# A fourth group of seven products in each feed-forward block, and weights split by whole tiles into buffers of their own

## The chip, the core and the metric

The kernel runs on one NeuronCore of a Trainium2 chip. The metric is the device time of one execution in microseconds (us). The engines work side by side, each through its own queue in program order: TensorE (PE) multiplies matrices into the PSUM banks, VectorE (DVE) and ScalarE (ACT) work on tiles element by element, GpSimd (POOL) and SyncE (SP) mostly issue DMAs here.

## The reference

Two layers, 256 tokens, width 1024, all in float32. Each layer is a feed-forward block, an attention block and a second feed-forward block:

```python
def swiglu(h, w_gate, w_up, w_down):
    return (jax.nn.silu(h @ w_gate) * (h @ w_up)) @ w_down
...
for l in range(DEPTH):
    x = x + 0.5 * swiglu(rms_norm(x, ffn1_norm[l]), ffn1_w_gate[l], ffn1_w_up[l], ffn1_w_down[l])
    h = rms_norm(x, mix_norm[l])
    proj = h @ w_in[l]                      # 2304 columns: windowed and differential attention
    ...
    x = x + jnp.concatenate([out_a, out_b], axis=-1) @ w_out[l]
    x = x + 0.5 * swiglu(rms_norm(x, ffn2_norm[l]), ffn2_w_gate[l], ffn2_w_up[l], ffn2_w_down[l])
return rms_norm(x, final_norm)
```

The feed-forward width is 2816: five groups of 512 columns (groups 0 to 4) and a rest of 256. There are four such blocks in the kernel, numbered 1 to 4 here in order of time.

## The kernel before

**Exact products from rounded parts.** Each float32 operand is split in two: a high part, cast to the matmul type (by ScalarE, `act.copy`), and a low part, the operand less the high part (by VectorE, `tensor_tensor` with subtract). A product is the sum of three matmuls: high by high, low by high, high by low. So each weight that is loaded costs ScalarE a cast and VectorE a subtract before TensorE can use it. `emit_split` does that.

**Steps of weights.** The list `specs` holds the weights in order of use, one `Step` for 1 MB (a raw tile of 128 x 2048 float32, 8 KB in each partition, `N_RAW` = 6 of them). A step is split in two halves of 128 x 1024. Each half takes two tiles of 4 KB (high, low) out of one pool, `s4`, of `N_S4` = 28, which holds the activations too (`blk`). `weights()` takes the next step, and calls `ahead`, which issues loads, splits and preparations of later steps, up to `look[0]` half steps further on: 8 in the feed-forward blocks, 6 in attention (`IN_FFN`, `IN_MIX`).

**A plain group** of 512 columns: 24 matmuls for each of four weight steps (gate and up, 512 rows each), 96 in all; Silu of gate on ScalarE, times up on VectorE (`hidden`). The group before is turned by TensorE (`turn`: eight transposes, then a split) and goes through two down steps (`down`, 24 matmuls each).

**A group of seven** (`by_seven`; groups 2, 3 and 4, `SEVEN`) computes gate and up as one 2 by 2 product of blocks (two blocks of tokens, two halves of the rows) with seven block products in place of eight, 12 matmuls each. Their weights are: a (gate, upper rows), b (up, upper rows), d, c (gate and up, lower rows), and the sums b + c, a + b, a + b + c, a + b + c + d, built in order in the tiles of b and a. The two additions of `gather` are DMAs that POOL issues and that add into the raw tile. The two of `plus` are VectorE additions of two raw tiles, in halves. So each group has nine steps, in the order of TensorE's work: p1 (a), p7 (b + c), p2 (d), p3 (c), the first down step, p5 (a + b), p6, p4, the second down step. VectorE then combines the products (`put`), and ScalarE applies Silu to g0 and g1. The activations need four sums too (`make_sums`), made once a block.

**The order in a block**: group 0 plain, group 1 plain, groups 2 to 4 by seven, the rest of 256 columns, the last down steps (`ffn_end`, `ffn_close`).

Outside attention all engines keep the program's order (`kept`), so what `ahead` emits is the order of VectorE and ScalarE.

Of the kernel before, what the change touches and what calls it, by code (L numbers as in the profile page):

```python
# [14 lines left out]
P = 128  # L15
# [13 lines left out]
N_RAW, N_S4 = 6, 28  # L29
IN_FFN, IN_MIX = 8, 6  # L30
SEVEN = (2, 3, 4)
# [3 lines left out]
def trunk(ctx: ExitStack, tc: tile.TileContext, x, n1, g1, u1, d1, nm, w_in, sink,  # L35
# [56 lines left out]
    class Step:  # L92
        def __init__(self, kn, n, moves, key=None, prep=None, src=None, free=None, behind=None):
# [21 lines left out]
    def seven(wg, wu, c0, downs):  # L115
# [21 lines left out]
        return [Step(4, 512, load(a), key=a, free=[]),  # L137
                Step(4, 512, load(b), key=b, behind=gather(c, b), prep=gather(b, a)),
                Step(4, 512, load(d), key=d, free=[]),
                Step(4, 512, load(c), key=c, free=[]),  # L140
                downs[0],
                Step(4, 512, None, src=a, free=[]),
                Step(4, 512, None, prep=plus(c, a), src=a, free=[c]),
                Step(4, 512, None, prep=plus(d, a), src=a, free=[a, d]),
                downs[1]]

    def emit_dma(i):
# [9 lines left out]
        if s.behind is not None:  # L157
            s.behind()
# [52 lines left out]

    def ahead(n):

        n = min(n, 2 * len(specs) - 1)
        while True:
            if at["split"] <= n and at["prep"] > at["split"] // 2:
                for _ in emit_split(*divmod(at["split"], 2)):
                    pass
                at["split"] += 1
            elif at["prep"] <= min(n // 2 + 1, len(specs) - 1) and at["dma"] > at["prep"] and \  # L220
                    (specs[at["prep"]].prep is None or at["split"] >= 2 * at["prep"]):
                if specs[at["prep"]].prep is not None:
                    specs[at["prep"]].prep()
                at["prep"] += 1
            elif at["dma"] < min(at["use"] + AHEAD, len(specs)) and (specs[at["dma"]].moves is None or len(raws) < N_RAW):
                if specs[at["dma"]].moves is not None:
                    for _ in emit_dma(at["dma"]):
                        pass
                at["dma"] += 1
            else:  # L230
                break
# [11 lines left out]
    for l in range(DEPTH):  # L243
        def ffn_specs(wg, wu, wd):
            down = lambda g, h: plain(wd[l], h * 512, 512, 4 * g, 4)
            for k0 in (0, 4):
                specs.extend(plain(w[l], 0, 512, k0, 4) for w in (wg, wu))
            for g in range(1, NGRP):
                downs = [down(g - 1, h) for h in range(2)]
                if g in SEVEN:  # L250
                    specs.extend(seven(wg[l], wu[l], g * 512, downs))
                else:
                    specs.extend(plain(w[l], g * 512, 512, k0, 4) for w in (wg, wu) for k0 in (0, 4))
                    specs.extend(downs)
# [24 lines left out]
        for k0 in (0, 2):  # L279
            def o_moves(t, k0=k0, wo=wo):  # L280
                return [(t[g * 64:g * 64 + 64], wo[g * 256 + k0 * 64:g * 256 + (k0 + 2) * 64].rearrange("(k p) n -> p k n", p=64))
                        for g in range(2)]
            specs.append(Step(2, D, o_moves))
        fine.update(range(mixed + 2, len(specs)))
# [5 lines left out]
    class Norm:  # L290


        def __init__(self, g0, sums=len(SEVEN) > 0):
# [39 lines left out]
        def make_sums(self):  # L333
# [5 lines left out]
            def make(x, y, op):  # L339
# [4 lines left out]
                act.copy(sm[:, :, 0:P], v)  # L344
                dve.tensor_tensor(sm[:, :, P:S], v, f(sm[:, :, 0:P]), op=ALU.subtract)
# [3 lines left out]
            s1 = make(b1, t1, ALU.subtract)  # L349
            yield  # L350
            s2 = make(s1, t0, ALU.add)
            yield
            make(t1, t0, ALU.subtract)
            yield
            make(b0, s2, ALU.subtract)
# [12 lines left out]
        def stats(self, n=512):  # L368
# [7 lines left out]
            dve.tensor_scalar_mul(self.hr, self.r, 0.5)  # L376

# [189 lines left out]
    def ffn(norm, aside=None, before=None, final=False):  # L567
# [31 lines left out]
        def by_seven(h, g):  # L599

# [6 lines left out]

            m1, m7 = flat(), flat()
            act.copy(m1, prod(norm.quarter(0, 0), weights()))
            act.copy(m7, prod(norm.summed(2), weights(held=True)))  # L610
            hT = turn(h, 2)
# [6 lines left out]
            p5 = prod(norm.summed(0), weights())  # L618
            late = g == max(SEVEN)
            p6 = prod(norm.summed(1), weights(look[0] - 5 if late else 0, late))  # L620
            u2 = put(flat(), p6, m1, ALU.subtract)
            u3 = put(m7, m7, u2, ALU.add)
            p4 = prod(norm.quarter(1, 1), weights(look[0] - 4 if late else 0, late))
            g1 = put(m1, p4, u3, ALU.subtract)
            w = weights(look[0] - 3 if late else 0)
            silu(g1, g1, 1)
            put(u3, u3, p5, ALU.subtract)
            put(u2, u2, p5, ALU.subtract)
            put(u2, u2, p3, ALU.add)
            up(h, u2, g0, 0)  # L630
            up(h, u3, g1, 1)
            down(hT, g - 1, 1, w)
            return h

        def turn(hs, n):
            out_ = []
            for i in range(n):
# [11 lines left out]
        def down(hT, g, h, w):  # L649
            tokens(accs[h], [None] * (2 * g) + hT, w, 4 * g, last=(FC - 1, G4 - 1) if final and h else FC - 1)  # L650

# [13 lines left out]
        tokens(gs, norm.xs, weights(), 4)  # L665
        g = gate(gs)
        tokens(us, norm.xs, weights(), 4)
        h = hidden(g, us)
        for n in range(1, NGRP):
            sums = norm.make_sums() if n + 1 == min(SEVEN, default=0) else iter(())  # L670
            if n in SEVEN:
                look[0] = IN_FFN - max(0, n - 2) if before is not take_x else IN_MIX
                h = by_seven(h, n)
                continue
            gs = [bank(), bank()]
            tokens(gs, norm.xs, weights(), 0)
            hT = turn(h, 2)
            norm.copies()
            tokens(gs, norm.xs, weights(), 4)
            g = gate(gs)  # L680
            next(sums, None)
            us = [bank(), bank()]
            for k0 in (0, 4):
                tokens(us, norm.xs, weights(), k0)
                next(sums, None)
            h = hidden(g, us)
            for hh in range(2):
                down(hT, n - 1, hh, weights())
                if hh == 0:
                    next(sums, None)  # L690

        gu = [bank(), bank()]
        tokens(gu, norm.xs, weights(), 0)
        hT = turn(h, 2)
        tokens(gu, norm.xs, weights(), 4)
        h = hidden(gate([b[:, 0:256] for b in gu]), [b[:, 256:512] for b in gu])
        if aside is not None:
            aside()
        return accs, hT, lambda: turn(h, 1)

    BY_TOKENS = [(k, t) for t in range(2) for k in range(2)]
    G4 = 4 * (NGRP - 1)

    def ffn_end(parts, last):

        accs, hT, rest = parts
        hT = [None] * (2 * (NGRP - 1)) + hT
        hE = []
        look[0] = IN_MIX
        w = {0: weights()}  # L710

        def group(h, order, a=None, c=slice(None), first=0):
            tokens(a or accs[h], hT, w[h], G4, first=first, last=last[h], order=order, cols=c)

        def tail(h, order=BY_TOKENS, a=None, c=slice(None)):
            tokens(a or accs[h], [None] * (2 * NGRP) + hE, w["rest"], 4 * NGRP, last=last[h], order=order, cols=c, h=h)

        group(0, [(k, t) for k in range(3) for t in range(2)])
        hE.extend(rest())
        group(0, [(3, t) for t in range(2)])  # L720
        w["rest"] = weights()
        w[1] = weights(2)
        return group, tail

    def ffn_close(parts, nxt):
        group, tail = ffn_end(parts, (FC - 1, G4 + 3))
        res = Residual(nxt, parts[0])
        group(1, [(0, t) for t in range(2)])
        tail(0)
        for t in range(2):  # L730
            res.add(0, t)
        tail(1)
        ahead(2 * at["use"] - 2 + look[0])
        group(1, [(1, t) for t in range(2)])
# [330 lines left out]
```

## Time and profile before

| | |
|---|---|
| median of 3 runs | 935.24 us (934.86 to 935.65) |
| profiled execution | 935.0 us, span 933.2 us |
| TensorE busy | 921.1 us, 4796 matmuls and transposes |
| VectorE busy | 759.9 us, 1074 instructions |
| ScalarE busy | 566.8 us, 889 instructions |
| DMA packets | 194.58 MB, mean 208 GB/s |
| 12 groups of seven | POOL issues 24 adding DMAs, median 10.5 us to landing |

The span is the profiled stretch from the first to the last instruction; the execution's time has 1.8 us more around it. All instructions carry line 50 (a helper issues them), so they are told apart by their tiles: `raw` is a loaded weight, `w` a part of a split one, `s` an `s4` tile, `ps` a PSUM bank. In a timeline a row has the start, the time and, in brackets, how long the engine stood before it and what ended that.

### The profile page before, as it was taken

How to read it: one execution, taken by the hardware profiler on the slowest of the kernel's cores; microseconds unless marked ns; L12 is line 12 of the kernel's file. 1: busy time of each engine (PE TensorE's matmuls, PEld its weight loads, DVE VectorE, ACT ScalarE, POOL GpSimd, SP SyncE). 2: the span in 40 equal slices, each digit the busy share in tenths (PEclk: the TensorE clock that was granted, in tenths of full speed). 3: DMA queues.
4: the chain of work that ended last, by engine and by line, in shares of the span. 5: the costliest groups of instructions: out<-in, count | busy, mean ns of one | idle time of the engine just before them, and what ended most of it. 6: DMA issues, size and time to landing. Idle time of an engine off the chain costs nothing.

```text
span 933.2 us, 12665 instructions
## 1 busy us (share of the span) xinstructions
PE 921.1 (99%) x4796; PEld 780.7 (84%) x4796; DVE 759.9 (81%) x1074; ACT 566.8 (61%) x889; POOL 55.0 (6%) x73
## 2 busy tenths in 40 slices
PE   8999999999999999999999999999999999999997
PEld 6888878799898888888888888888999888888886
DVE  6759999869866588999776799996697566799994
ACT  7837576457745657576475466565577476466561
POOL 0400000000000001000000000000000000001011
PEclk9999999999999999999999999999999999999999
DMA  9996898827335858797767597887462367597831
GB/s 334 347 233 200 251 271 270 235 97 217 131 93 178 271 135 261 191 269 271 240 236 204 140 299 203 238 283 218 144 187 91 136 213 198 145 299 203 248 113 46
DMA packets 110893, 194.58 MB, mean 208 GB/s; under 512 B 3566, under 2 KB 31280, under 8 KB 110832
## 3 DMA queue, kind: packets, MB, share of 16 engines
q1 hardware_dynamic: 96528, 166.74, 52.8%
q0 software_dynamic: 12928, 25.46, 15.4%
q10 hardware_dynamic: 1376, 1.57, 0.5%
q8 instruction: 37, 0.61, 0.3%
q14 instruction: 24, 0.20, 0.1%
HBM read 192.71 MB, written 1.05 MB: 208 GB/s over the span
## 4 chain that ended last, share of the span: by engine, by line
PE 93%; DVE 4%; issue 1%; DMA 0%; ACT 0%; POOLq 0%; POOL 0%; ACTq 0%; DVEq 0%
PE ps L50 93%; DVE w L50 3%; DVE s L50 1%; DMA xk<-in_x_dram 0%; DVE tmp L50 0%; DVE raw L50 0%; ACT w L50 0%; DVE distA L50 0%; DVE xk L50 0%; DVE distB L50 0%; POOLq L1060 0%; POOL rf L50 0%; ACTq L50 0%; DVE lsum L50 0%; DVEq L50 0%
## 5 line engine op out<-in xcount | busy, mean ns | idle before, releaser
L50 PE MATMUL ps<-w,s 128*128 128x512 f32 (+1 forms) x2754 | 641.3, 391 | 1.2 <-DVE s L50 1.1
L50 PEld LDWEIGHTS ps<-w,s 128*128 128x128 f32 x2754 | 511.3, 188 | 107.5 <-DVE s L50 1.6
L50 DVE TENSOR_TENSOR w<-raw,w 128x1024 fp32r<-128x1024 f32 (+1 forms) x440 | 460.4, 1093 | 59.3 <-ACT w L50 58.1
L50 ACT CAST w<-raw 128x1024 fp32r<-128x1024 f32 (+1 forms) x440 | 391.1, 948 | 91.9 <-DVE raw L50 69.6
L50 PE MATMUL ps<-w,q 128*128 128x512 f32 x432 | 101.9, 389 | 0.0
L50 PEld LDWEIGHTS ps<-w,q 128*128 128x128 f32 x432 | 81.1, 188 | 16.8
L50 PE MATMUL ps<-s,w 128*128 128x256 f32 x672 | 84.0, 285 | 0.0
L50 PEld LDWEIGHTS ps<-s,w 128*128 128x128 f32 x672 | 81.7, 191 | 1.1
L50 ACT ACTIVATE s<-ps,gcol 128x256 fp32r<-128x256 f32 (+1 forms) x80 | 31.5, 488 | 47.0 <-PE ps L50 47.0
L50 DVE TENSOR_TENSOR raw<-raw,raw 128x1024 f32<-128x1024 f32 x48 | 56.5, 1219 | 0.0
L50 ACT CAST s<-ps 128x512 fp32r<-128x512 f32 x48 | 26.1, 593 | 46.5 <-PE ps L50 46.5
L50 POOL DMA_DIRECT2D raw<-in_ffn_w_up_dram x24 | 31.1, 1296 | 352.9 <-DVE w L50 166.5
L50 DVE TENSOR_TENSOR s<-ps,s 128x512 fp32r<-128x512 f32 x48 | 31.0, 684 | 25.1 <-ACT s L50 25.1
L50 PE MATMUL ps<-ident,s 128*128 128x128 f32 x304 | 39.9, 274 | 0.6 <-DVE s L50 0.6
L50 PEld LDWEIGHTS ps<-ident,s 128*128 128x128 f32 x304 | 35.0, 141 | 5.9 <-DVE s L50 1.4
L50 ACT ACTIVATE tmp<-tmp,r 128x512 f32<-128x512 f32 x24 | 17.3, 722 | 34.0 <-DVE tmp L50 34.0
L50 ACT ACTIVATE s<-s,negm 128x256 f32<-128x256 f32 x64 | 31.9, 500 | 6.3 <-DVE negm L50 6.1
L50 PE MATMUL ps<-w,v 128*128 128x512 f32 x144 | 34.6, 389 | 0.0
L50 ACT CAST q<-tmp 128x512 fp32r<-128x512 f32 x20 | 12.4, 621 | 35.3 <-DVE tmp L50 35.2
L50 PEld LDWEIGHTS ps<-w,v 128*128 128x128 f32 x144 | 27.0, 188 | 5.6
L50 DVE SCALAR_TENSOR_TENSOR s<-ps,gcol,s 128x256 fp32r<-128x256 f32 x48 | 20.3, 478 | 12.5 <-ACT s L50 12.4
L50 ACT COPY tmp<-ps 128x512 f32<-128x512 f32 x24 | 14.0, 584 | 22.6 <-PE ps L50 22.5
(106 smaller groups left out, 427.0 us busy)
## 6 DMA issues: line engine op xcount, KB each, us to landing
raw<-in_ffn_w_down_dram SPq DMA_DIRECT2D x44, 1024.0 KB, 5.4
raw<-in_ffn_w_gate_dram SPq DMA_DIRECT2D x39, 1024.0 KB, 6.0
raw<-in_ffn_w_up_dram SPq DMA_DIRECT2D x39, 1024.0 KB, 5.4
raw<-in_ffn_w_up_dram POOLq DMA_DIRECT2D x24, 1024.0 KB, 10.5
raw<-in_w_in_dram SPq DMA_DIRECT2D x14, 1024.0 KB, 5.1
raw<-in_ffn_w_gate_dram SPq DMA_DIRECT2D x8, 512.0 KB, 6.4
raw<-in_ffn_w_up_dram SPq DMA_DIRECT2D x8, 512.0 KB, 7.3
raw<-in_w_in_dram SPq DMA_DIRECT2D x8, 512.0 KB, 6.3
```

The source lines that it names most:

```text
L50: ins = issue(*a, **k)
```

## The change

- Group 1 goes by seven as well. The rest of 256 columns moves to the place between group 0 and group 1, and `make_sums` stands around it. The order of the block is: group 0, the rest, groups 1 to 4 by seven, then the rest's down step (`tail`) and the last two.
- The 28 shared tiles become 8 tiles of 8 KB for weights (tag `w`, `N_W`), and 12 of 4 KB for activations. A step takes two of the 8 KB tiles, one high and one low, and so four steps fit. The steps of the groups of seven and the down steps but the last two are `whole`: one cast and one subtract of 128 x 2048.
- `plus` adds a whole raw tile in one instruction.
- The order in which steps are split is decided by a model of the times (`clk`, `chain`, `fill`, `passed`), and `take` looks no further than the step itself. The loads have an order of their own (`order`).
- The adding DMA into b is held until the statistics of the norm are there (`held`, `flush`).

```diff
-N_RAW, N_S4 = 6, 28
-IN_FFN, IN_MIX = 8, 6
-SEVEN = (2, 3, 4)
+N_RAW, N_W, N_S4 = 6, 8, 12
+IN_FFN, IN_MIX = N_W - 1, N_W - 1
...
         def plus(x, to):
             def prep():
-                for h in (0, 2):
-                    x_, t_ = [raws[i][:, h:h + 2] for i in (x, to)]
-                    dve.tensor_tensor(t_, t_, x_, op=ALU.add)
+                dve.tensor_tensor(raws[to], raws[to], raws[x], op=ALU.add)
             return prep
...
         if s.behind is not None:
-            s.behind()
+            behind.append(s.behind)
+            if not held[0]:
+                flush()
...
-            loaded[i] = Split(i)
-        shape = (P, 8, P) if s.n == 256 else (P, 2, 512)
-        hi, lo = [s4.tile(list(shape), F32R, tag="s4", name=nm_("w")) for _ in range(2)]
-        loaded[i].parts.append((hi, lo))
+            loaded[i] = w = Split(i)
+            shape = {256: (P, 2, 8, P), 512: (P, 2, 2, 512), D: (P, 2, 2, 512)}[s.n]
+            w.both = [wp.tile(list(shape), F32R, tag="w", bufs=N_W, name=nm_("w")) for _ in range(2)]
+            if s.whole:
+                hi, lo = [t.rearrange("p a k n -> p (a k) n") for t in w.both]
+                act.copy(hi, raw)
+                dve.tensor_tensor(lo, raw, f(hi), op=ALU.subtract)
+        loaded[i].parts.append([t[:, j] for t in loaded[i].both])
+        if s.whole:
...
+    def fill(until):
+
+        while clk["dve"] < until and at["split"] < min(2 * at["use"] + LIVE, 2 * len(specs)) and act_once(at["split"]):
+            pass
+        while load_once():
+            pass
...
+    def chain(cost, release=None):
+
+        r = clk["pe"] if release is None else release
+        fill(r)
+        clk["dve"] = max(clk["dve"], r) + cost
...
-            for g in range(1, NGRP):
-                downs = [down(g - 1, h) for h in range(2)]
-                if g in SEVEN:
-                    specs.extend(seven(wg[l], wu[l], g * 512, downs))
-                else:
-                    specs.extend(plain(w[l], g * 512, 512, k0, 4) for w in (wg, wu) for k0 in (0, 4))
-                    specs.extend(downs)
             for k0 in (0, 4):
                 def gu_moves(t, k0=k0, ws=(wg[l], wu[l])):
                     return [(t[:, :, h * 256:h * 256 + 256], rows(w, FF - 256, 256, k0, 4)) for h, w in enumerate(ws)]
                 specs.append(Step(4, 512, gu_moves))
-            specs.append(down(NGRP - 1, 0))
+            for g in range(1, NGRP):
+                specs.extend(seven(wg[l], wu[l], g * 512, [down(g - 1, h) for h in range(2)]))
             specs.append(plain(wd[l], 0, D, 4 * NGRP, 2))
-            specs.append(down(NGRP - 1, 1))
+            specs.extend(down(NGRP - 1, h) for h in range(2))
...
-        def by_seven(h, g):
+        def by_seven(hT, h, g):
...
-            p2 = prod(norm.quarter(0, 1), weights())
+            p2 = product(norm.quarter(0, 1))
+            chain(0.65)
             g0 = put(flat(), p2, m1, ALU.add)
-            p3 = prod(norm.summed(3), weights())
             silu(g0, g0, 0)
-            down(hT, g - 1, 0, weights())
+            p3 = product(norm.summed(3))
+            down_(0)
```

More of the change, by code (lines that the diff above doesn't have):

```diff
@@ L210, in trunk @@
     at = dict(use=0, dma=2, prep=2, split=4)
-    def ahead(n):
[L214 to L229, printed above, removed]
-            else:
-                break
+    order = []
@@ new lines, in trunk, with act_once @@
+    fetched = set()
+    LIVE = N_W
+    SPLIT, ADD, PROD = 1.1, 1.1, 2.72
+    clk = dict(pe=0.0, dve=0.0)
+    ready, freed = {}, {}
+    def act_once(n):
+        i, j = divmod(at["split"], 2)
+        if at["split"] <= n and at["prep"] > i:
+            for _ in emit_split(i, j):
+                pass
+            clk["dve"] = max(clk["dve"], freed.get(at["split"] - LIVE, 0.0)) + SPLIT * (2 - 2 * j if specs[i].whole else 1)
+            ready[at["split"]] = clk["dve"]
+            at["split"] += 1
+            return True
+        p = at["prep"]
+        if p <= min(n // 2 + 1, len(specs) - 1) and (specs[p].moves is None or p in fetched) and \
+                (specs[p].prep is None or at["split"] >= 2 * p):
+            if specs[p].prep is not None:
+                specs[p].prep()
+                clk["dve"] += 2 * ADD * (specs[p].moves is None)
+            at["prep"] += 1
+            return True
+        return load_once()
@@ new lines, in load_once @@
+    def load_once():
+        k = at["dma"]
+        if k < len(order) and k < at["use"] + AHEAD and len(raws) < N_RAW:
+            for _ in emit_dma(order[k]):
+                pass
+            fetched.add(order[k])
+            at["dma"] += 1
+            return True
+        return False
+    def ahead(n):
+        while act_once(min(n, 2 * len(specs) - 1)):
+            pass
+    def fill(until):
+        while clk["dve"] < until and at["split"] < min(2 * at["use"] + LIVE, 2 * len(specs)) and act_once(at["split"]):
+            pass
+        while load_once():
+            pass
@@ L233, in weights, with passed, take @@
+    def passed(i, t):
+        for h in (2 * i, 2 * i + 1):
+            clk["pe"] = max(clk["pe"], ready.get(h, 0.0)) + t / 2
+        freed[2 * i] = freed[2 * i + 1] = clk["pe"]
+    def chain(cost, release=None):
+        r = clk["pe"] if release is None else release
+        fill(r)
+        clk["dve"] = max(clk["dve"], r) + cost
+    def take():
+        i = at["use"]
+        at["use"] += 1
+        ahead(2 * i + 1)
+        w = loaded[i]
+        w.held = True
+        return w
     def weights(less=0, held=False):
@@ L283, in trunk @@
             specs.append(Step(2, D, o_moves))
+        order.extend(range(mixed, len(specs)))
         fine.update(range(mixed + 2, len(specs)))
@@ L290, in trunk, with __init__ @@
     class Norm:
-        def __init__(self, g0, sums=len(SEVEN) > 0):
+        def __init__(self, g0, sums=True):
             self.g0, self.xs, self.sums = g0, [], sums
@@ L347, in make @@
                 return v
-            s1 = make(b1, t1, ALU.subtract)
+            yield from make(t1, t0, ALU.subtract)
             yield
-            s2 = make(s1, t0, ALU.add)
+            s1 = yield from make(b1, t1, ALU.subtract)
             yield
-            make(t1, t0, ALU.subtract)
+            s2 = yield from make(s1, t0, ALU.add)
             yield
-            make(b0, s2, ALU.subtract)
+            yield from make(b0, s2, ALU.subtract)
             yield
@@ L565, in late, with ffn @@
                 self.nxt.stats()
-    def ffn(norm, aside=None, before=None, final=False):
+    def ffn(norm, before=None):
         def silu(out_, acc, t):
@@ L630, in by_seven @@
             up(h, u2, g0, 0)
+            chain(0.7)
             up(h, u3, g1, 1)
-            down(hT, g - 1, 1, w)
-            return h
+            clk["up"] = clk["dve"]
+            down_(1)
+            return hs, h
         def turn(hs, n):
             out_ = []
-            for i in range(n):
+            for i in (range(n) if isinstance(n, int) else n):
                 sl = halves(bank())
@@ L649, in down @@
         def down(hT, g, h, w):
-            tokens(accs[h], [None] * (2 * g) + hT, w, 4 * g, last=(FC - 1, G4 - 1) if final and h else FC - 1)
+            tokens(accs[h], [None] * (2 * g) + hT, w, 4 * g, last=-1)
         gs, us = [bank(), bank()], [bank(), bank()]
@@ L664, in ffn, with part, sum_step @@
         before(2)
-        tokens(gs, norm.xs, weights(), 4)
+        clk.update(pe=0.0, dve=0.0, up=0.0)
+        ready.clear()
+        freed.clear()
+        def part(accs_, k0):
+            w = take()
+            tokens(accs_, norm.xs, w, k0)
+            passed(w.i, 2 * PROD)
+        def sum_step():
+            next(sums)
+            clk["dve"] += 0.65
+            fill(clk["dve"] + 0.5)
+            next(sums)
+            clk["dve"] += 0.65
+        part(gs, 4)
+        fill(clk["pe"])
@@ L666, in ffn @@
         g = gate(gs)
-        tokens(us, norm.xs, weights(), 4)
+        part(us, 4)
+        chain(1.4)
         h = hidden(g, us)
[L669 to L690, printed above, removed]
@@ L692, in ffn @@
-        gu = [bank(), bank()]
-        tokens(gu, norm.xs, weights(), 0)
+        norm.copies()
+        sums = norm.make_sums()
+        gu = [bank(), bank()]
+        part(gu, 0)
+        for _ in range(2):
+            fill(clk["dve"] + 1.0)
+            sum_step()
+        clk["pe"] = max(clk["pe"], clk["up"]) + 0.9
+        chain(1.3, clk["pe"] + 0.6)
         hT = turn(h, 2)
-        tokens(gu, norm.xs, weights(), 4)
+        for _ in range(2):
+            sum_step()
+        part(gu, 4)
@@ L696, in ffn, with tail @@
+        chain(0.9)
         h = hidden(gate([b[:, 0:256] for b in gu]), [b[:, 256:512] for b in gu])
+        hE, h = by_seven(hT, h, 1)
+        for n in range(2, NGRP):
+            h = by_seven(None, h, n)[1]
+        held[0] = True
+        look[0] = IN_MIX
+        return accs, hE, lambda: turn(h, 2)
+    BY_TOKENS = [(k, t) for t in range(2) for k in range(2)]
+    ALL = [(k, t) for k in range(4) for t in range(2)]
+    G4 = 4 * (NGRP - 1)
+    def tail(accs, hE, w, h, last=-1):
+        tokens(accs, [None] * (2 * NGRP) + hE, w, 4 * NGRP, last=last, order=BY_TOKENS, h=h)
@@ L697, in ffn, with group, ffn_close @@
+    def group(accs, hT, w, order, c=slice(None), first=0):
+        tokens(accs, [None] * (2 * (NGRP - 1)) + hT, w, G4, first=first, last=G4 + 3, order=order, cols=c)
+    def ffn_close(parts, nxt, aside=None):
+        accs, hE, turn_ = parts
+        res = Residual(nxt, accs)
+        we = weights(3, True)
+        for h in range(2):
+            tail(accs[h], hE, we, h)
+        hT = turn_()
         if aside is not None:
             aside()
-        return accs, hT, lambda: turn(h, 1)
-    BY_TOKENS = [(k, t) for t in range(2) for k in range(2)]
@@ L702, in trunk @@
[L702 to L729, printed above, removed]
+        group(accs[0], hT, weights(), ALL)
         for t in range(2):
             res.add(0, t)
-        tail(1)
-        ahead(2 * at["use"] - 2 + look[0])
-        group(1, [(1, t) for t in range(2)])
+        w = weights()
+        group(accs[1], hT, w, ALL[:4])
         for j in range(2):
@@ L737, in ffn_close @@
         res.squares(0)
-        group(1, [(2, t) for t in range(2)])
-        group(1, [(3, t) for t in range(2)])
+        group(accs[1], hT, w, ALL[4:])
         for t in range(2):
@@ L1029, in trunk @@
         acc = bank()[:, 0:256]
-        cols = slice(c, c + 256)
-        group(1, [(k, 1) for k in range(4)], [None, acc], cols, G4)
-        tail(1, [(k, 1) for k in range(2)], [None, acc], cols)
+        group([None, acc], hT, w, [(k, 1) for k in range(4)], slice(c, c + 256), G4)
         close(1, 512 + c, 256, acc)
```

100 lines of the change are left out of this document (73 added, 27 removed).

## The prediction

> **What bounds the kernel now.** I read the page first: the busy shares, then the chain that ended last.
>
> ```profile
> PE 921.1 (99%) x4796; PEld 780.7 (84%) x4796; DVE 759.9 (81%) x1074; ACT 566.8 (61%) x889; POOL 55.0 (6%) x73
> PE 93%; DVE 4%; issue 1%; DMA 0%; ACT 0%; POOLq 0%; POOL 0%; ACTq 0%; DVEq 0%
> ```
>
> TensorE carries 93% of the chain. But the mean share hides stages, so next I read one group of seven of the first feed-forward block: first the busy time by window, from one group's product p5 to the next group's.
>
> ```profile
> core 0: us, PE busy (x) PEld busy (x) DVE busy (x) ACT busy (x) POOL busy (x), PEclk, DMA share, GB/s
> 81.83:112.65 30.82, 30.82 (x142) 25.61 (x140) 30.65 (x32) 19.78 (x23) 1.73 (x2) 1.00 0.93 270
> ```
>
> TensorE needs 30.82 us for a group, and VectorE is busy for 30.65 of them: these groups are balanced on a knife's edge. The timelines of VectorE and then ScalarE show how.
>
> ```profile
> 77.58 2.35 DVE L50 TENSOR_TENSOR raw<-raw,raw 128x1024 f32<-128x1024 f32 x2
> 79.85 0.68 DVE L50 TENSOR_TENSOR tmp<-ps,tmp 128x512 f32<-128x512 f32 x1
> 80.45 2.35 DVE L50 TENSOR_TENSOR w<-raw,w 128x1024 fp32r<-128x1024 f32 x2
> 82.72 2.35 DVE L50 TENSOR_TENSOR raw<-raw,raw 128x1024 f32<-128x1024 f32 x2
> 85.14 6.91 DVE L50 TENSOR_TENSOR w<-raw,w 128x1024 fp32r<-128x1024 f32 x6
> ...
> 109.80 2.36 DVE L50 TENSOR_TENSOR raw<-raw,raw 128x1024 f32<-128x1024 f32 x2
> ```
>
> ```profile
> 78.84 2.19 ACT L50 CAST w<-raw 128x1024 fp32r<-128x1024 f32 x2 [2.81 <-DVE raw L50]
> 84.05 5.99 ACT L50 CAST w<-raw 128x1024 fp32r<-128x1024 f32 x6 [2.40 <-DVE raw L50]
> ```
>
> VectorE adds one weight quarter to another in two halves (77.58). ScalarE starts casting at 78.84, just behind the first half, so its first cast is ready when VectorE has done the second half, and VectorE never stands. VectorE's own period is 109.80 - 77.58 = 32.2 us, 1.4 more than TensorE's; the lead of four weight steps, built in the plain groups, pays for it.
>
> The sizes by form give the prices:
>
> ```profile
> L50 DVE TENSOR_TENSOR w<-raw,w 128x1024 fp32r<-128x1024 f32 x336 | 394.0, 1220 | 52.6 <-ACT w L50 51.5
> L50 ACT CAST w<-raw 128x1024 fp32r<-128x1024 f32 x336 | 333.4, 1051 | 89.3 <-DVE raw L50 69.6 <-DMA raw<-in_ffn_w_up_dram 17.6 <-DMA raw<-in_ffn_w_gate_dram 0.5
> L50 DVE TENSOR_TENSOR w<-raw,w 128x512 fp32r<-128x512 f32 x104 | 66.5, 685 | 6.7 <-ACT w L50 6.5
> L50 ACT CAST w<-raw 128x512 fp32r<-128x512 f32 x104 | 58.0, 617 | 2.6 <-DMA raw<-in_ffn_w_up_dram 1.3 <-DMA raw<-in_ffn_w_gate_dram 1.1
> ```
>
> No row has 2048 elements. From 512 to 1024 a VectorE subtract grows by 0.535 us and a ScalarE cast by 0.434; twice that on top of 1024 gives 2.29 and 1.92 us at 2048. Back to back, six take 6.91, so 1.14 each at 1024 and 2.20 at 2048.
>
> **TensorE's work.** A plain group has 96 matmuls of 512 columns for gate and up, a group of seven 7 x 12 = 84. One more such group in each of four blocks takes 48 out. The timeline of TensorE has the price:
>
> ```profile
> 87.28 11.04 PE L50 MATMUL ps<-w,s 128*128 128x512 f32 x48
> 107.21 5.60 PE L50 MATMUL ps<-w,s 128*128 128x512 f32 x24
> ```
>
> The last matmul's own length is 0.39 (the page's mean), so 47 steps take 10.65, 0.227 each: **-10.9**. They are on the path, since TensorE is.
>
> **A steady group after.** VectorE's work: 9 whole splits and 2 whole adds of 2.20 = 24.3; the products' sums, ups and turns, 7.1 (from one start to the next in the same timeline: two sums 1.3, g1 0.6, three sums and two ups 3.4, turns 1.2, g0 0.6). Sum 31.3, less than 32.2. Now the waits, following program order, with 0 where VectorE starts the low part of the fifth step's weight (a plus the gathered b, "a'"):
> - a' split to 2.3, whole add to 4.5. ScalarE can cast only now: to 6.5. Nothing lies between on VectorE: **2.0 idle**. Split to 8.8.
> - Add to 11.0, cast to 13.0 (**2.0 idle**), split to 15.3. These splits release p6 and p4.
> - Down split to 17.5, two sums to 18.7, next group's a to 20.9, g1 to 21.5, three sums and two ups to 24.7. ScalarE: Silu of g1 to 22.3, then casts of b, d, c with the copy of m1 between, to 28.3. VectorE splits b, d, c to 31.4, turns to 32.6. ScalarE's copy of m7, turn casts and down cast end at 32.9: **0.4 idle**; down split to 35.2, g0 to 35.9.
> - Next is a' again, whose cast stands on ScalarE behind Silu of g0, which needs g0: 0.7 and 1.9: **2.6 idle**, to 38.4.
>
> So 31.3 + 7.0 = 38.4 us a group, against TensorE's 30.8. The other groups' order differs little: 39.1 from the first to the second (the down cast stands ahead of the turns), 39.5 from the third to the fourth (m1's copy ahead of the d cast).
>
> **The first group of seven.** T0 is TensorE's end on group 0. Eight 8 KB buffers are four steps, so d's cast waits until the first step of the last 256 columns has left its buffer, T0 + 5.4: cast to 7.4, split to 9.7. Behind it, in order: two sums of activations, each 0.7 + ScalarE's cast 0.6 + 0.7, with VectorE standing meanwhile (13.7), turns (15.0), two more sums (19.0), ups of the 256 columns (19.8), c 23.7, down 26.1, turn 26.7, a' 28.9, g0 29.5, add, cast, split 36.0, add, cast, split 42.5, down 44.7. TensorE's last product of the group ends at 50.5. Its own work from T0 is 180 matmuls and 12 transposes (8 take 1.03 with overlap, so 0.11 each), 42.1: **8.4 lost**. Then 39.1 + 38.4 + 39.5 - 3 x 30.8 = 24.6, less 0.8 for a fourth group without a next one's a: **32.2 a block, 128.6 in all**.
>
> **Three smaller terms.** (1) In blocks 1 and 3 the new hold keeps b's gathering DMA on POOL until the norm's statistics.
>
> ```profile
> DMA to landing us min/median/max: 8.3/10.5/15.6
> ```
>
> Issued some 5 us ahead of T0, it lands near T0 + 6, and b's split stands on VectorE before the ups of group 0, which TensorE's turn needs: 6 and 5 us later, **11** (bounds 4 and 18; in blocks 2 and 4 it is issued early, at nothing). (2) The ends: the last 512-column group's turn comes alone instead of inside products (1 to 1.5 a block), and whole-step splits stand before the residual adds; in block 1 the attention constants (3.3 us of VectorE, 172.8 to 176.3) too: 6 + 2.5 + 2.5 + 1.5 = **12.5** (4 to 20). (3) Attention: 12 activation buffers were in effect left by 28 less 16 for four steps, so nothing there; but splits come four halves at a time. TensorE shows no gap there before, so it can't gain much; VectorE's waits of up to 5.2 us there are cover: **2** (0 to 10). The 2048 casts themselves and the extra gathers (2 MB a block; the DMA share falls with the longer period) hide under the waits.
>
> **Sum.** Against the profiled execution's 935.0 (span 933.2; the runs' median is 935.24): 935.0 - 10.9 + 128.6 + 11 + 12.5 + 2 = **1078**.
>
> [...] The granted clock is 1.00 in the group's window, with no idle. After, TensorE idles for 7.6 us a group, at most 1.9 at a stretch, with two matmuls between the two longest. [...]
>
> **Rivals.**
> - *The lead hides it, TensorE stays the bound* (faster): VectorE's 31.3 of work is less than the 32.2 that the lead bears now. Four steps of lead are 4 x 30.8 / 9 = 13.7 us, 3.4 for each of four groups, so it decides from a VectorE period of 30.8 + 3.4 = 34.2, that is with waits below 2.9 a group in place of 7.0. Then 935.0 - 10.9 = 924. For it: ScalarE is busy 64% of the window (19.78 of 30.82), so it has room. Against it: ScalarE can't cast a sum that VectorE has not finished, and the add is now one instruction. Chance 0.06.
> - *Only the waits after the adds count*: the Silu of g0 and a's cast get ahead of VectorE. Period 31.3 + 4.0 = 35.3, 4.5 a group, 18 a block: 935.0 - 10.9 + 72 + 12 for the small terms = 1008. Against it: g0 is VectorE's last operation before a'. Chance 0.09.
> - *The clock drops in the gaps*: TensorE's slowest stretch before is its start, 24 matmuls in 7.64 us, 0.318 each. At that, 132 take 42, with turns 43, which is more than 38.4: 4.6 x 16 = 74 more, 1152. [...] Chance 0.05.
> - That the change doesn't do what it says is excluded by the instruction order: 16 groups of 84 matmuls are there.
>
> **Numbers.** My forecast has 0.80. Its own bounds: low, a block at 28 and the small terms at their lows (4, 4, 0), 935 - 11 + 112 + 8 = 1044; high, gathers landing at 15.6, 1.3 more a group, 34 a block, and all highs (18, 20, 10): 935 - 11 + 136 + 48 = 1108. The three rivals are outside with 0.20, so the range is 1044 to 1108. Measurement tells 0.2% from no change: faster 0.06, same 0.01, slower 0.93.
>
> **What would show it.** In the profile after: VectorE idle about 2 us, released by ScalarE's w, before two of every eleven 2048-element operations, and 2.6 before a'; a period of 38 to 39 us in the groups; TensorE's share near 85% (910 of 1076) and VectorE's near 75% (760, 4 x 15 for a group of seven in place of a plain one, less 12 x 0.9, over 1076); 2048 forms of 2.29 and 1.92 us. I'm wrong if TensorE stays at 99%, if the period is below 36 us, or if the granted clock falls.

## The result, and the profile after

The changed kernel takes 1112.67 us (median of 4 runs, 1108.87 to 1115.99), beside 935.44 for the kernel before: a ratio of 1.1891, interval 1.1875 to 1.1906. The profiled execution has a span of 1112.1 us. The prediction said 1078, with a range of 1044 to 1108: the direction and VectorE's waits came as forecast, the size was 35 us short, and the range missed it by 5.

The page after, engines and chain:

```profile
PE 990.6 (89%) x4742; PEld 805.4 (72%) x4742; DVE 819.2 (74%) x966; ACT 581.2 (52%) x777; POOL 63.7 (6%) x81
PEclk9899899889999989889899899899999999889889
PE 56%; DVE 21%; ACT 13%; issue 5%; DMA 4%; ACTq 0%; POOLq 0%; POOL 0%; DVEq 0%
```

TensorE runs 54 instructions fewer and is busy 70 us longer. The second row has part of the reason: the granted clock is below full in many slices of the run (mean 0.936, before 0.999). The chain now goes through VectorE and ScalarE for a third of the span.

The groups by form, with the idle time ahead of them:

```profile
L49 DVE TENSOR_TENSOR w<-raw,w 128x2048 fp32r<-128x2048 f32 x144 | 326.8, 2289 | 166.0 <-ACT w L49 166.0
L49 ACT CAST w<-raw 128x2048 fp32r<-128x2048 f32 x144 | 270.8, 1907 | 169.0 <-DVE raw L49 82.0 <-PE ps L49 70.5 <-DMA raw<-in_ffn_w_up_dram 12.2
L49 DVE TENSOR_TENSOR raw<-raw,raw 128x2048 f32<-128x2048 f32 x32 | 73.3, 2291 | 1.0
```

The prices of 2048 elements, which no row showed before, are 2.29 and 1.91 us, as extrapolated (2.29 and 1.92). VectorE stands 166 us ahead of whole splits, all of it for ScalarE's casts.

VectorE's timeline over one steady group of block 1, then ScalarE's:

```profile
107.38 2.29 DVE L49 TENSOR_TENSOR w<-raw,w 128x2048 fp32r<-128x2048 f32 x1 [2.59 <-ACT w L49]
109.70 2.29 DVE L49 TENSOR_TENSOR raw<-raw,raw 128x2048 f32<-128x2048 f32 x1
114.03 2.29 DVE L49 TENSOR_TENSOR w<-raw,w 128x2048 fp32r<-128x2048 f32 x1 [2.04 <-ACT w L49]
...
120.69 4.49 DVE L49 TENSOR_TENSOR w<-raw,w 128x2048 fp32r<-128x2048 f32 x2 [2.04 <-ACT w L49]
...
138.46 2.29 DVE L49 TENSOR_TENSOR w<-raw,w 128x2048 fp32r<-128x2048 f32 x1 [1.24 <-ACT w L49]
```

```profile
112.10 1.90 ACT L49 CAST w<-raw 128x2048 fp32r<-128x2048 f32 x1 [4.76 <-DVE raw L49]
...
136.03 0.59 ACT L49 COPY tmp<-ps 128x512 f32<-128x512 f32 x1 [2.33 <-PE ps L49]
136.51 1.92 ACT L49 CAST w<-raw 128x2048 fp32r<-128x2048 f32 x1
```

The waits of the prediction stand where it put them: 2.0 us behind each add (109.70 ends at 112.0, the cast runs to 114.0), 2.6 ahead of the split of a' (the weight a + b). One is new: 1.24 us at 138.46, for a cast that stands in ScalarE's queue behind the copy of m1 (the product p1, copied out of its bank), and that copy waits for TensorE's product p1.

TensorE's timeline shows why p1 is late, in block 1 and in the same group of block 2 (at 446):

```profile
114.06 0.73 PE L49 MATMUL ps<-w,q 128*128 128x512 f32 x2 [1.31 <-ACT w L49]
116.38 2.55 PE L49 MATMUL ps<-w,q 128*128 128x512 f32 x10 [1.59 <-DVE w L49]
120.71 1.05 PE L49 MATMUL ps<-w,s 128*128 128x512 f32 x2 [1.78 <-ACT w L49]
123.04 12.95 PE L49 MATMUL ps<-w,s 128*128 128x512 f32 x46 [1.28 <-DVE w L49]
```

```profile
446.34 4.64 PE L49 MATMUL ps<-w,q 128*128 128x512 f32 x10 [1.59 <-DVE w L49]
...
453.00 10.72 PE L49 MATMUL ps<-w,s 128*128 128x512 f32 x46 [1.10 <-DVE w L49]
```

The 46 matmuls behind p4's first two (rest of p4, a down step, p1 of the next group) take 12.95 us in one place and 10.72 in the other. Three windows ahead of the two falls (columns: length, busy time of PE, PEld, DVE, ACT, POOL, then the granted clock, DMA share and GB/s):

```profile
112.00:121.00 9.00, 4.31 (x17) 2.67 (x16) 4.89 (x3) 4.14 (x3) 0.00 (x0) 1.00 0.50 147
117.54:120.95 3.41, 1.62 (x8) 1.05 (x7) 1.37 (x2) 2.19 (x2) 0.00 (x0) 1.00 0.34 76
441.80:445.21 3.41, 1.60 (x6) 0.68 (x4) 1.37 (x2) 1.90 (x1) 0.00 (x0) 1.00 0.60 175
```

After 9 us in which TensorE was busy for 4.3, the clock is halved for 6.8 us (120.95 to 127.78), and then full again. In block 2 the halved stretch begins at 445.2, and the ten matmuls of p6 pay for it (4.64 us in place of 2.55), which have time to spare.

The last two rows show what the two falls have in common, and it isn't the 9 us: in the 9 us ahead of the second (436.21 to 445.21), TensorE stood for 1.81. The trace's records of the granted clock change only on one grid, every 3.413 us from 8.31 on. All 29 falls of this run come at the end of a grid window in which TensorE was busy for half or less of the time (at most 0.50; 0.48 and 0.47 in the two rows). Of the 253 windows after which the clock stayed at 1.00, only two were below 0.50 (0.45 and 0.48; the boundary can't be read more sharply, since the matmuls' ends are modelled). The clock came back 28 times, each time after a window with 0.91 or more, and stayed halved after windows with up to 0.82. So in the groups a halved stretch lasts one window (3.41 us) or two (6.83), and the waits of a group, which is not a multiple of 3.41 us long, meet the grid now one way and now another.

### The profile page after: what moved, and what is told of

It reads as the page before. It is cut to its first block, busy times and chain, and to the rows that moved or that the text cites. A ratio compares the mean times of both kernels' runs of the same rounds, so it can differ in the third digit from the quotient of the medians.

```text
span 1112.1 us, 12355 instructions
## 1 busy us (share of the span) xinstructions
PE 990.6 (89%) x4742; PEld 805.4 (72%) x4742; DVE 819.2 (74%) x966; ACT 581.2 (52%) x777; POOL 63.7 (6%) x81
## 4 chain that ended last, share of the span: by engine, by line
PE 56%; DVE 21%; ACT 13%; issue 5%; DMA 4%; ACTq 0%; POOLq 0%; POOL 0%; DVEq 0%
PE ps L49 56%; DVE w L49 12%; ACT w L49 11%; DVE raw L49 4%; DMA raw<-in_ffn_w_up_dram 3%; DVE tmp L49 2%; DVE s L49 1%; ACT s L49 1%; ACT tmp L49 1%; DVE q L49 1%; ACT q L49 1%; DVE xk L49 0%; DMA xk<-in_x_dram 0%; ACTq L49 0%; DVE distA L49 0%
## 5 line engine op out<-in xcount | busy, mean ns | idle before, releaser
L49 PE MATMUL ps<-w,s 128*128 128x512 f32 x2508 | 638.3, 413 | 52.0 <-DVE w L49 27.2
L49 DVE TENSOR_TENSOR w<-raw,w 128x2048 fp32r<-128x2048 f32 (+2 forms) x320 | 477.8, 1528 | 213.8 <-ACT w L49 213.2
L49 PEld LDWEIGHTS ps<-w,s 128*128 128x128 f32 x2508 | 492.6, 200 | 177.4 <-DVE w L49 38.3
L49 ACT CAST w<-raw 128x2048 fp32r<-128x2048 f32 (+2 forms) x320 | 399.4, 1294 | 232.0 <-PE ps L49 124.6
L49 PE MATMUL ps<-w,q 128*128 128x512 f32 x576 | 158.0, 424 | 39.9 <-DVE w L49 23.1
L49 PEld LDWEIGHTS ps<-w,q 128*128 128x128 f32 x576 | 114.6, 204 | 76.5 <-DVE w L49 31.0
L49 DVE TENSOR_TENSOR raw<-raw,raw 128x2048 f32<-128x2048 f32 x32 | 73.3, 2291 | 1.0
L49 PE MATMUL ps<-w,v 128*128 128x512 f32 x192 | 46.7, 391 | 0.1
L49 ACT ACTIVATE s<-ps,gcol 128x256 fp32r<-128x256 f32 (+1 forms) x80 | 31.2, 478 | 26.5 <-PE ps L49 26.5
L49 ACT ACTIVATE s<-s,negm 128x256 f32<-128x256 f32 x64 | 31.8, 500 | 9.2 <-DVE negm L49 9.1
L49 DVE TENSOR_TENSOR tmp<-ps,tmp 128x512 f32<-128x512 f32 x48 | 32.9, 686 | 3.1 <-PE ps L49 2.7
L49 DVE TENSOR_TENSOR tmp<-tmp,ps 128x512 f32<-128x512 f32 x48 | 31.6, 685 | 1.1
## 6 DMA issues: line engine op xcount, KB each, us to landing
raw<-in_ffn_w_up_dram POOLq DMA_DIRECT2D x32, 1024.0 KB, 10.3
```

The costliest lines, as they stand in the source:

```text
L49: ins = issue(*a, **k)
```

## Where the 179 us went, by landmarks

The norm's transposes mark where a block begins and ends on TensorE. From the last pair of one norm to that of the next, after less before: block 1 +51.8, attention +4.4, block 2 +37.9, block 3 +40.1, attention +4.3, block 4 +41.1 (179.6, less 0.6 by which block 1 began earlier). Within a block, T0 to the first whole add, the three periods from group to group (first add to first add), and the rest to the block's end can be read the same way. Summed over the four blocks, the changed kernel takes 197.5 us from the norm to the first add, 490.3 for the periods and 194.9 for the rest. The experiments below are read by these landmarks as well as by their time.

## The experiments

**Idle matmuls in TensorE's waits.**

```diff
-        def prod(xo, w):
+        def prod(xo, w, warm=0):
             acc = bank()
+            for _ in range(warm):
+                pe.matmul(acc, lhsT=norm.xs[0][:, 0, 0:P], rhs=norm.xs[0][:, 0], start=True, stop=True)
...
-            p6 = product(norm.summed(2))
+            p6 = product(norm.summed(2), 14)
-            p4 = product(norm.quarter(1, 1))
+            p4 = product(norm.quarter(1, 1), 14)
```

> The changed kernel with 14 idle matmuls (activation tile by itself, into the bank that the product clears at its start) ahead of the products p6 and p4 of each group of seven: 28 x 0.227 = 6.4 us more TensorE work a group, in the time in which it stands now. No wait of VectorE is removed. Theory (the half clock behind these waits makes the next group's p1 late, and with it ScalarE's copy of m1 and VectorE's d and c splits): granted clock 0.99 to 1.00, the 46 matmuls behind p4's first two in 10.5 us and not 12.3 to 13.3, group periods 39 and not 40 to 42.5, 22 us less in the periods and about 6 in the blocks' ends: 1085 us. Rival (TensorE has room, so the half clock costs nothing and the missing 36 us are VectorE's and ScalarE's own): 1112 us, the periods as before, whatever the clock.

Measured: 1095.26 us, ratio 1.1704 (1.1684 to 1.1723), mean clock 0.985. In a steady group of block 2:

```profile
434.38:473.58 39.20, 37.85 (x169) 30.41 (x168) 31.83 (x22) 20.06 (x15) 2.59 (x2) 1.00 0.78 215
```

448 matmuls more, and 17 us less. The three periods of a block sum to 118.8 to 119.7 us, where they were 121.8 to 124.0, and the clock is 1.00 in all twelve. The rival falls: the half clock costs 17 us, of the 28 that were expected of it.

**The same ahead of p4 alone** (p6 without them).

> The changed kernel with the 14 idle matmuls ahead of p4 alone: TensorE's two waits at p6 (1.3 and 1.6 us with two matmuls between) stay, those at p4 are filled. Theory (the clock goes by how much TensorE stands within some 8 us, 4.7 of 8.3 us ahead of the fall, not by one long wait): half of it is filled, the clock stays at 1.00 in the groups (mean 0.98), 1095 us as with both filled. Rival (two waits of 1.3 and 1.6 us are enough): clock 0.94 to 0.95, 1105 to 1113 us.

Measured: 1097.13 us, ratio 1.1731 (1.1704 to 1.1757), mean clock 0.973. Eight of the twelve periods have a granted clock of 1.00 and four 0.96; the waits at p6 alone, 1.3 and 1.6 us, sometimes halve the clock and mostly don't. So the theory of 8 us came near in its forecast (1095 us, mean clock 0.98), but it isn't shown to be the cause: four periods fell although the waits at p4 were filled. What sets these four apart from the other eight is not shown.

**Sums in halves.** The three sums' weights are split in halves, the adds are done in halves.

```diff
-                dve.tensor_tensor(raws[to], raws[to], raws[x], op=ALU.add)
+                for h in (0, 2):
+                    x_, t_ = [raws[i][:, h:h + 2] for i in (x, to)]
+                    dve.tensor_tensor(t_, t_, x_, op=ALU.add)
...
-                Step(4, 512, None, src=a, free=[], whole=True),
-                Step(4, 512, None, prep=plus(c, a), src=a, free=[c], whole=True),
-                Step(4, 512, None, prep=plus(d, a), src=a, free=[a, d], whole=True),
+                Step(4, 512, None, src=a, free=[]),
+                Step(4, 512, None, prep=plus(c, a), src=a, free=[c]),
+                Step(4, 512, None, prep=plus(d, a), src=a, free=[a, d]),
```

> The changed kernel with the three sums' weights (a + b and the two VectorE sums) split in halves of 1024 again and the VectorE adds in halves. Theory: both 2.0 us waits behind the adds go, 0.6 us of VectorE's work comes back (five operations in halves, 0.1 each), and with the gaps of TensorE gone the clock stays at 1.00, so the extra 1.4 us a group go too: period 35.0 to 35.5, 16 groups by about 5: 1030 us. If the clock falls all the same: 1055. Rival (the adds are off the path, ScalarE's casts or the buffers set the period): over 1095 us.

Measured: 1036.28 us, ratio 1.1079 (1.1061 to 1.1098). VectorE in block 1:

```profile
105.54 2.36 DVE L49 TENSOR_TENSOR w<-raw,w 128x1024 fp32r<-128x1024 f32 x2 [1.73 <-ACT w L49]
107.82 2.35 DVE L49 TENSOR_TENSOR raw<-raw,raw 128x1024 f32<-128x1024 f32 x2
110.23 2.36 DVE L49 TENSOR_TENSOR w<-raw,w 128x1024 fp32r<-128x1024 f32 x2
```

Adds and splits follow each other without a gap, the period is 35.0 to 35.4, and the granted clock 1.00 in a steady group (416.85 to 451.89). Of the 76 us that go, the twelve periods give 67 (14 of them are the half clock, by the run with idle matmuls) and the stretches behind each block's last first add 17, while the first adds come 8 later. At full clock a middle period falls from 39.2 to 35.1. The two waits of 2.04 are nearly all of that, but not the edit's only effect: the wait ahead of a' is 1.73 us in place of 2.59, since VectorE needs only the first half of its cast to begin, and one of 0.51 stands ahead of the next down split.

**Adds in halves, casts whole** (only the first hunk of the diff above).

> The changed kernel with the VectorE adds in halves again, casts and subtracts whole. Theory (the 2.0 us wait is ScalarE's whole cast, which needs both halves of the sum, so the size of the add is not what costs): two adds of 2.29 become four that take 2.35 a pair, the waits stay 2.0: 1112 to 1115 us. Rival (the long add is the cost): 1080 us or less.

Measured: 1113.55 us, ratio 1.1890 (1.1866 to 1.1915): nothing.

```profile
115.30 2.29 DVE L49 TENSOR_TENSOR w<-raw,w 128x2048 fp32r<-128x2048 f32 x1 [2.04 <-ACT w L49]
```

So it isn't the size of the add that costs, but that the cast behind it is one piece, and so can't begin under the add.

**Silu of g0 behind the cast of a'.**

```diff
-            silu(g0, g0, 0)
             p3 = product(norm.summed(3))
             down_(0)
+            ahead(2 * at["use"])
+            silu(g0, g0, 0)
```

> The changed kernel with Silu of g0 issued behind the first down step and the cast of a + b in ScalarE's queue. Theory: the 2.6 us wait ahead of the a + b split goes and nothing takes its place: 16 x 2.6 = 42 less, 1071 us, both 2.0 us waits and the half clock as they are. Rival (the wait moves to the next operation that needs ScalarE, or to the up that needs g0): 1100 us or more.

Measured: 1082.27 us, ratio 1.1546 (1.1509 to 1.1584), 30 us less at the median and 39 less in the profiled execution. Its periods are 36.5 to 37.3 where the clock is 1.00, 2.7 below those of the run with idle matmuls, and up to 40.0 where it fell (to a mean of 0.91). So the whole wait is on the path, and at full clock nothing takes its place. The expectation was too high: only 12 of the 16 groups have this wait, since the first of a block shows none.

**No hold of the adding DMA into b.**

```diff
-    behind, held = [], [True]
+    behind, held = [], [False]
...
-        held[0] = True
         look[0] = IN_MIX
```

> The changed kernel without the hold of the adding DMA into b: it is issued as soon as both loads are, in all four blocks. Theory (the hold makes the gather late): the first add of block 1's first group of seven comes at T0 + 29 to 30 and not T0 + 39.4, block 3's at T0 + 29 to 30 and not 31.1: 12 us less, 1100 us. Rival (in block 1 the weights' loads themselves are late, since all queues are full at the start, 339 GB/s in the first slice): block 1 gains under 4 us, 1107 or more.

Measured: 1105.27 us, ratio 1.1820 (1.1760 to 1.1880). Block 3 gains its 2.1 us, block 1 half a microsecond (13.96 to 70.30 between its landmarks, 56.3; with the hold 56.8). In block 1 the hold costs next to nothing: the adding DMA goes out at 28.18 without it and at 28.05 with it. The twelve periods are 7.6 us shorter in all, in groups in which the clock stayed up; these don't show what the hold is worth.

What is late in block 1 shows in its timelines with the hold, GpSimd's and ScalarE's:

```profile
28.05 1.47 POOL L49 DMA_DIRECT2D raw<-in_ffn_w_up_dram  x1 [1.33 <-DMA raw<-in_ffn_w_up_dram]
```

```profile
30.11 1.90 ACT L49 CAST w<-raw 128x2048 fp32r<-128x2048 f32 x1 [4.23 <-DMA raw<-in_ffn_w_gate_dram]
...
41.57 1.90 ACT L49 CAST w<-raw 128x2048 fp32r<-128x2048 f32 x1 [6.98 <-DMA raw<-in_ffn_w_up_dram]
```

GpSimd has computed the norm's statistics by 26.7. What it waits for until 28.05 is the weights' own loads. The sum lands at 41.6. Meanwhile the core's DMAs move 313 GB/s (between 28.0 and 41.6), where the mean over the run is 182.

**Without block 1's first adding DMA** (b alone in place of b + c; `gather` skips its first call).

> The changed kernel without the very first adding DMA (b + c of block 1's first group of seven is b alone; the product p7 of that group is computed from b). Theory (block 1's start is late because this DMA goes out at 28 us, when the loads of b and c have landed, and takes 13.6 us behind a full queue): ScalarE casts b some 10 us earlier, the first add stands at T0 + 29 to 31 and not T0 + 39.4: 9 to 10 us less, 1103 us. Rival (the loads themselves, full queues in the first 30 us, are what is late): under 4 us less, 1109 or more.

Measured: 1107.41 us, ratio 1.1832 (1.1799 to 1.1864). The first add comes at 63.18, T0 + 32.8. So of the 10.4 us by which block 1 is late, 6.6 are this DMA, and 3.8 remain without it, where the wait for a load at 30.11 above stays (3.28 there). Both theories had a part.

**Fewer half steps ahead in attention**: `IN_MIX = 5`, not 7.

> The changed kernel with splits 5 half steps ahead in place of 7 in attention and in the ends of the blocks (IN_MIX). Theory (at 7 a fourth step's casts stand on ScalarE, waiting for a buffer, ahead of the norm's operands and the residual's adds): the stretch from the second-but-last to the last norm transposes at the end of attention falls from 10.9 us to 6.6 as before the change, twice, and the blocks' ends gain 1 to 3 us each: 1097 us. Rival (the buffers themselves make TensorE wait there): attention as it is or longer, 1112 us or more.

Measured: 1099.75 us, ratio 1.1751 (1.1732 to 1.1769). ScalarE at the end of attention, in the changed kernel and here:

```profile
342.67 1.04 ACT L49 CAST w<-raw 128x1024 fp32r<-128x1024 f32 x1 [4.34 <-PE ps L49]
343.62 1.56 ACT L49 ACTIVATE s<-ps,gcol 128x256 fp32r<-128x256 f32 x4
```

```profile
337.02 0.84 ACT L49 ACTIVATE s<-ps,gcol 128x256 fp32r<-128x256 f32 x2 [3.69 <-PE ps L49]
```

A fourth step's cast stood 4.3 us for a buffer, with the operands of the next norm behind it. Without it TensorE's stretch there is 6.6 us again, as before the change, both times. Of the blocks' ends, for which 1 to 3 us each were expected, only block 1's got shorter, by 2.5 us; the others are as they were.

**The adds alone, in the kernel before**: its 24 additions as whole instructions, all else as it was.

> The kernel before with one edit: the two VectorE additions of each of its 12 groups of seven as one instruction of 2048 elements, splits in halves as they are. Theory (VectorE stands 1.1 us after each, until ScalarE has cast a half): its period goes from 32.2 to 34.4, but the lead of four steps, 13.7 us for three groups, bears up to 30.8 + 4.6 = 35.4: 935 to 939 us. Rival (the lead is spent already): 12 x 2.2 = 26 more, 961 us.

Measured: 954.92 us, ratio 1.0202 (1.0185 to 1.0219).

```profile
87.34 6.90 DVE L50 TENSOR_TENSOR w<-raw,w 128x1024 fp32r<-128x1024 f32 x6 [1.20 <-ACT w L50]
```

The theory falls. Block 1's period goes from 32.2 to 34.1, near the 34.4 expected, but the 12 groups pay 1.6 us each on average, nearly all of these 1.9. In block 1 TensorE stands for 1.0 us in the first period and 2.2 in the second: the lead was all but spent before.

**The fourth group alone, in the kernel before**: `SEVEN = (1, 2, 3, 4)`, with the activations' sums made at once behind group 0; shared tiles, halves and look-ahead as they were, the rest of 256 columns at the end.

> The kernel before with one part of the change alone: group 1 goes by seven too, with the 28 shared tiles, halves and look-ahead as they were; the rest of 256 columns stays at the end, and the activations' sums are made at once behind group 0. Theory (VectorE's period of 32.2 us binds a group of seven as soon as no plain group builds a lead for it): 10.9 less for the matmuls; the first group loses 2 to 4 us a block behind the sums, the three others 1.4 each, block 1's start up to 10 for loads that come late: 950 to 965 us. Rival (the lead hides it and TensorE stays the bound): 924 to 930 us.

Measured: 980.06 us, ratio 1.0477 (1.0460 to 1.0494), 15 over the range expected. Block 1 is 21.1 us longer than before, the others 7.1, 6.6 and 8.2. The first group waits for its sums:

```profile
342.46 5.79 PE L50 MATMUL ps<-w,q 128*128 128x512 f32 x12 [3.99 <-ACT q L50]
```

4.0 us of wait, and the 12 matmuls behind it take 5.8 instead of 2.9: the half clock again (0.50 in that stretch). The periods are 32.1 to 34.0. So of the whole change's 177 us, a fourth group with its sums costs 44 by itself, though it takes 48 matmuls away.

**Four edits together** (sums in halves, late Silu, no hold, 5 ahead in attention), and then with both halves of a' cast ahead of Silu.

> Four edits together on the changed kernel: sums in halves, Silu of g0 behind the cast of a + b, no hold, 5 half steps ahead in attention. Theory (the terms add): period 35.1 less the 1.7 us that half_sums still shows ahead of the a + b split, 33.4; half_sums' 1036 less 16 x 1.7 = 27, less 2 for block 3's gather, less 9 for attention and 4 to 8 for the ends: 992 us. Still slower than before the change, since VectorE's work of 31.9 us a group is over TensorE's 30.8, and the first group, block 1's start and the turns cost the rest. Rival (with the waits gone the lead of four steps hides the rest, TensorE bounds the groups): period 30.8 to 31.5, below 965 us.

> As the four edits together, but both halves of a + b are cast ahead of Silu of g0 (there the second half still stood behind it, and VectorE waited 0.6 us for it): period 34.0 to 33.3, 16 x 0.6 = 9 less than 1012: 1003 us. Rival (the waits for ScalarE's copies take its place): 1010 or more.

Measured: 1012.10 us, ratio 1.0810 (1.0794 to 1.0826), and 996.14, ratio 1.0646 (1.0628 to 1.0664). The first was 20 over its expectation. The second half of a' still stood behind Silu (0.6 us a group, periods 33.9 to 34.3), which is some 10 of the 20; casting it ahead gave 16. The rest was not taken apart. The second was 7 under. Its steady group:

```profile
400.20:433.44 33.24, 31.23 (x141) 25.24 (x140) 32.00 (x28) 20.44 (x18) 2.60 (x2) 1.00 0.86 240
```

VectorE is busy for 32.0 of 33.2 us, TensorE for 31.2. These edits give back 117 of the 177 us. What is left of the period is nearly all VectorE's own work, and no version here beats the kernel before.

## Why the prediction was right in kind and short in size

By its own steps, in us of the profiled execution (1112.1 against a predicted span of 1076.2):

- *Waits of a steady group.* Right: 2.0, 2.0, 0.2 to 0.5 and 2.6 stand in the trace, and the edits that take them away give time back (76 us for the halves, with all that hung on the two waits behind the adds, 30 to 39 for Silu's).
- *The periods.* Sized at 39.1, 38.4 and 39.5, 117.0 a block; measured 121.8 to 124.0, 22.3 more in all. 14 of these are the half clock, by the run with idle matmuls. The other 8 stay at full clock (39.6, 39.2, 40.0): in the middle group VectorE's work was put at 31.3 and is 31.8, its idle time at 7.0 and is 7.4.
- *The first group.* First add expected at T0 + 29.5, measured 29.0 in blocks 2 and 4: 2 less in all.
- *The held DMA.* 11 forecast, 12.5 measured (T0 + 39.4 in block 1 and + 31.1 in block 3, against 29.0). Nearly the size, but by luck, since the cause was another: 10.4 of it is block 1, where without the hold nothing is gained but 0.5; the adding DMA goes out 2.4 us ahead of T0 and not 5, behind the loads, and lands 11.1 behind it and not 6. Only block 3's 2.1 is the hold.
- *The ends.* 7.7 more than the prediction implies from the last group's first add to the block's end; 3 of it is the half clock, the rest was not taken apart.
- *Attention.* 2 forecast, 8.7 measured. The prediction took VectorE's waits there as cover. What counted was ScalarE's queue: a cast waiting for a buffer ahead of the next norm's operands.
- *The clock.* This is the step that failed. The sum has no term for a fall of the clock, which was 1.00 in the window read of the kernel before. A fall in the gaps was a rival with 0.05, the author's estimate, priced for the whole of the groups at 74. It came in a milder form: a halved clock for some 6.8 us of most groups (0.50 from 120.95 to 127.78), worth 17 in all, since TensorE had room for a part of it. The prediction gave the gaps as at most 1.9 us at a stretch, and such gaps were enough: the longest ahead of the fall at 120.95 is 1.78 us, and TensorE was busy for 1.62 of that window's 3.41 us. Kept at full clock by idle matmuls, the kernel took 1095, within the range. The rival's price was wrong too: it took 0.318 us a matmul from the kernel's start, and at half clock ten took 4.64, some 0.45 each. The prediction's own mark, "I'm wrong if ... the granted clock falls", was hit.

So of the 36 us missing, 17 are the clock, 7 attention, 8 the periods' own sizes, and some 4 the ends and the start. And the rival in which the lead bears waits of up to 2.9 us a group was wrong in its price too: in the kernel before, 1.9 more a group cost 1.6.

## What to carry to other kernels

When two engines hand one tile back and forth (add, cast, subtract), the size of the piece decides whether they overlap: two halves of 1024 hid a cast that one piece of 2048 exposed, at nearly the same price (2.36 us for a subtract in two halves, 2.29 in one piece). Ask of every wait on one engine what stands behind it in its queue (the copy of m1, the norm's operands), and count short waits of TensorE together: in the changed kernel waits of at most 1.8 us each left it busy for half or less of a window of 3.41 us, and the clock fell to 0.50. So a fix that shortens them can bring back more than their length: of the 67 us that the halves gave back in the periods, 14 are the half clock. A lead in buffers is only cover if it is not spent already; one edit that lengthens the period a little shows which.

## What the runs showed of the hardware

In the changed kernel's trace the granted clock is either 1.00 or 0.50, and it changes only on a grid of 3.413 us. Each of its 29 falls came after a grid window in which TensorE was busy for 0.50 of the time or less (in 25 of the 29 no single wait is above 1.8 us), though the clock also stayed at 1.00 after two windows of 0.45 and 0.48; it came back after windows with 0.91 or more. What a fall cost there depended on which matmuls it met: periods of the second group of seven were 39.2 us at a mean granted clock of 0.91 (the halved stretch over p6) and 40.3 at 0.92 (over p4). 14 idle matmuls ahead of each of the two waiting products, written into a bank that is cleared anyway, kept it at 1.00 in all twelve periods that were read. And a 1 MB adding DMA behind the loads of the first 30 us took 13.4 us from its issue at 28.05 to landing, where the median over the run is 10.3.
